# Seven block products for eight in the feed-forward stage of a two-layer decoder trunk

## The chip, the cores and the metric

The kernel runs as one program on one core of one Trainium2 chip. The metric is device time in microseconds (us) of one execution: the median of the runs shown.

## The reference

Two layers over 256 tokens of width 2048, all in float32. A layer has a mixer (one input projection, a causal convolution branch, an attention branch, gates, an output projection), then a SwiGLU feed-forward part of hidden width 5632, then a gated embedding. The change lies in the feed-forward part and in how weights are loaded:

```python
hf = rmsnorm(x, norm_ffn_g[i])
gate, up = jnp.split(hf @ w_gate_up[i], 2, axis=-1)
x = x + (jax.nn.silu(gate) * up) @ w_down[i]
```

## The kernel before, in words

**Tiling.** The 256 tokens are two blocks of 128 (`b` in 0, 1); the contraction is cut into tiles of 128 (`k`), and the output columns into chunks of 512. One weight chunk `w[g]` holds four k-tiles of 512 columns, 128 x 2048 numbers, and comes by one DMA.

**Precision.** Every float32 operand is split into a high part `h` (rounded to float32r by ACT) and a low part `l` (the rest, by DVE), and a product is three matmuls: high x high, high x low, low x high (lines 168 to 170). For activations, which stand transposed as the stationary operand, `halves` (line 183) does the split; for weights, which stream, `load` (line 131) does it: L147 on ACT writes `wh`, L148 on DVE writes `wl`, each 128 x 1024, two of each for a DMA. Both kinds have 4 buffers, the raw weights 3 (of 128 x 2048).

**A chunk.** `chunk` (line 154) loads one weight group after another and issues, for each k-tile and token block, three matmuls into two PSUM banks: 12 matmuls for each half group ("block" below), 24 for a group of four k-tiles. Between groups `run()` (line 81) issues what has been queued meanwhile, for instance the transposes of a finished hidden tile.

**Feed-forward.** The loop at line 676 goes over three parts of 3, 4 and 4 column chunks of the hidden width. In a part, each chunk `c` takes one gate and one up projection over 16 k-tiles (96 matmuls each), the gate's activation (L682, L683) and product (L686), and queues `operand` (line 202), which turns the hidden chunk by eight transposes (L199) and splits it (L186, L187) into four k-tiles. After a part's chunks, the down projection runs for each of four column chunks over 4 x nch k-tiles and is added to the residual stream `xt` (L666). Ahead of the stage, while the output projection runs (line 668 on), `advance` queues `Norm.turn` (line 226), which turns a finished column block of `xt` and splits it with the norm's gains (L189 on ACT, L190 on DVE).

**Order.** The program is written in one sequence; the tile framework's scheduler decides the order on each engine at build time, and each engine works strictly in that order. SP issues all weight DMAs in order, each as soon as a raw buffer is free.

Of the kernel before, what the change touches and what calls it, by code (L numbers as in the profile page):

```python
# [10 lines left out]
F32 = mybir.dt.float32  # L11
# [5 lines left out]
P = 128  # L17
# [17 lines left out]
PAIRS = 23  # L35
CONV = 7
# [7 lines left out]
def trunk(ctx, tc, xT, xR, pT, wI, wF, wC, wA, wOut, wGU, wD, wPG, wPP, vec, bF, gF, out):  # L44
# [4 lines left out]
    raws = pool("raws", 3)  # L49
    whs = pool("whs", 4)  # L50
    wls = pool("wls", 4)
    tmps = pool("tmps", 8)
# [78 lines left out]
    def load(src, n=2048, hook=None):  # L131
        raw = raws.tile([P, 2048], F32, tag="raw", name=f"raw{next(uid)}")
        if hook is None:
            nc.sync.dma_start(raw[:, :n], src)
        else:
            nc.sync.dma_start(raw[:, :512], src[:, :512])
            nc.sync.dma_start(raw[:, 512:1024], src[:, 512:1024])
            hook()
            nc.sync.dma_start(raw[:, 1024:], src[:, 1024:])
        parts = []  # L140
        step = 1024 if hook is None else 512
        for lo in range(0, n, 1024):
            h = whs.tile([P, 1024], F32R, tag="wh", name=f"wh{next(uid)}")
            l = wls.tile([P, 1024], F32R, tag="wl", name=f"wl{next(uid)}")
            for o in range(0, 1024, step):
                e = o + step
                act.activation(h[:, o:e], raw[:, lo + o : lo + e], AF.Copy)  # L147
                dve.tensor_tensor(l[:, o:e], raw[:, lo + o : lo + e], h[:, o:e].bitcast(F32), op=ALU.subtract)  # L148
            parts.append((h, l))
        return parts  # L150
# [3 lines left out]
    def chunk(groups, xs, acc, hook=None):  # L154
        n = sum(len(ks) for _, ks in groups)
        done = 0
        for src, ks in groups:
            parts = load(src, 512 * len(ks), hook)
            hook = None
            while not all(k in xs for k in ks):  # L160
                assert turns or tasks
                run()
            for j, k in enumerate(ks):
                h, l = parts[j // 2]
                cs = slice((j % 2) * 512, (j % 2 + 1) * 512)
                for b in range(2):
                    xh, xl = xs[k][:, b * P : (b + 1) * P], xs[k][:, S + b * P : S + (b + 1) * P]
                    pe.matmul(acc[b], lhsT=xh, rhs=h[:, cs], start=(done == 0), stop=False)  # L168
                    pe.matmul(acc[b], lhsT=xh, rhs=l[:, cs], start=False, stop=False)  # L169
                    pe.matmul(acc[b], lhsT=xl, rhs=h[:, cs], start=False, stop=(done == n - 1))  # L170
                done += 1
# [30 lines left out]
    def operand(xs, k0, src):  # L202
        for half, pt in turned(src):
            o = pair(F32R)
            halves(o, pt)
            for kk in range(2):
                xs[k0 + 2 * half + kk] = o[:, kk, :]

    class Norm:


        def __init__(self, gcol):
            self.gcol, self.xs = gcol, {}
            self.ss = small(8)
# [11 lines left out]
        def turn(self, n):  # L226
            for half, pt in turned(lambda b: xt[:, b, n * 512 : (n + 1) * 512]):
                o = pair(F32R)
                for kk in range(2):
                    k = 4 * n + 2 * half + kk  # L230
                    halves(o[:, kk, :], pt[:, kk, :], self.gain(k))
                    self.xs[k] = o[:, kk, :]
# [47 lines left out]
    def take(q, lo=0, hi=4):  # L280
        for k in range(lo, hi):
            if k % 2 == 0:
                o = pair(F32R)
                norm.xs[4 * q + k], norm.xs[4 * q + k + 1] = o[:, 0, :], o[:, 1, :]
            halves(
                norm.xs[4 * q + k], xin[q].rearrange("p a b -> p (a b)")[:, k * S : (k + 1) * S],
                norm.gain(4 * q + k),
            )
# [23 lines left out]
    for i in range(L):  # L312
# [7 lines left out]
        def project(c, hook=None):  # L320
            return chunk(by_four(wI[i, c]), norm.xs, banks(), hook)
# [164 lines left out]
        def scores(hd):  # L486
# [39 lines left out]
            def pv():  # L526
# [8 lines left out]
                o_att[hd] = o_pairs[hd // 2][:, hd % 2, :]  # L535
                halves(o_att[hd], po[:, :S])
# [20 lines left out]
        def conv_norm():  # L557
# [30 lines left out]
            def finish(c):  # L588
# [8 lines left out]
                o_conv[c] = r["o"][:, c % 2, :]  # L597
                halves(o_conv[c], t)
# [31 lines left out]
        def attended(n):  # L630
            return chunk(by_four(wA[i, n], 2), o_att, banks())
# [24 lines left out]
        for n in range(N4):  # L656
            t = gate_a[n]
            gated_by(t, chunk(by_four(wC[i, n], 2), o_conv, banks()))
# [9 lines left out]
        norm = Norm(g_ffn)  # L668
        for n in range(N4):
            residual(n, chunk(by_four(wOut[i, n]), merged, banks()))  # L670
            advance(norm, n)
# [4 lines left out]
        for part, nch in enumerate(FFN_PARTS):  # L676
            hid = {}
            for c in range(c0, c0 + nch):
                pg = chunk(by_four(wGU[i, 2 * c]), norm.xs, banks())
                t = [tmp() for _ in range(2)]  # L680
                for b in range(2):
                    act.activation(t[b], pg[b], AF.Sigmoid, scale=norm.r(b))  # L682
                    dve.scalar_tensor_tensor(t[b], pg[b], norm.r(b), t[b], op0=ALU.mult, op1=ALU.mult)  # L683
                pu = chunk(by_four(wGU[i, 2 * c + 1]), norm.xs, banks())
                for b in range(2):
                    dve.scalar_tensor_tensor(t[b], pu[b], norm.r(b), t[b], op0=ALU.mult, op1=ALU.mult)  # L686
                turns.append(lambda c=c, t=t, hid=hid: operand(hid, 4 * c, lambda b: t[b]))
            for n in range(N4):
                groups = [(wD[i, n, c], range(4 * c, 4 * c + 4)) for c in range(c0, c0 + nch)]
                residual(n, chunk(groups, hid, banks()))  # L690
                if part == len(FFN_PARTS) - 1:
                    advance(after, n)
            c0 += nch
            if part == len(FFN_PARTS) - 2:
# [4 lines left out]
                ps = {k: po[:, k, :] for k in range(2)}  # L699
# [5 lines left out]
        def embed(n):  # L705
            return chunk([(wPP[i, n], range(2))], ps, [bank_ms() for _ in range(2)])
# [6 lines left out]
        for n in range(N4):  # L713
            e = embed(n)
            acc = chunk(by_four(wPG[i, n]), norm.xs, banks())
# [84 lines left out]
```

## Time and profile before

| | |
|---|---|
| median of 3 runs | 2903.79 us (2902.66 to 2904.2) |
| the profiled execution's own time | 2902.9 us |
| its span, first to last instruction | 2900.8 us |
| mean granted TensorE clock | 0.998 |
| busy: TensorE (PE), DVE, ACT | 99%, 60%, 47% of the span |
| DMA, mean over the span | 187 GB/s |

Spans of the profile are read against 2900.8 us; the 2.1 us around the span belong to every execution. A matmul's listed duration (0.39 us) is longer than the distance to the next one, since matmuls are pipelined; what one costs is the distance between starts.

### The profile page before, as it was taken

The numbers are of one execution on the slowest core, as the hardware profiler recorded it, in microseconds if no ns is written. First come the engines' busy times: TensorE is split into PE (matmuls) and PEld (weight loads), VectorE is DVE, ScalarE is ACT, GpSimd is POOL, SyncE is SP. The second block draws the span as 40 slices with busy tenths as digits, with TensorE's granted clock in tenths as the row PEclk, the third lists the DMA queues.
The fourth block names the chain that finished last, engine by engine and source line by source line (L and its number), as shares of the span: only waits on it lengthen the run. The fifth ranks groups of instructions, "written<-read, shape, count | busy, mean of one in ns | idle before, by whom it ended". The sixth has DMA issues, their size and how long they took to land.

```text
span 2900.8 us, 32675 instructions
## 1 busy us (share of the span) xinstructions
PE 2876.6 (99%) x13004; PEld 2381.2 (82%) x13004; DVE 1751.8 (60%) x2264; ACT 1356.2 (47%) x1642; POOL 9.5 (0%) x40
## 2 busy tenths in 40 slices
PE   8999999999999999999999999999999999999998
PEld 6888888888888888888888888888888888888886
DVE  5997745555555555555569966465555555455554
ACT  5445744444444434445554456444443444344444
POOL 0000000000000000000000000000000000000000
PEclk9999999999999999999999999999999999999999
DMA  7554455555555555555555544555555555555553
GB/s 271 174 186 163 170 193 189 189 185 188 193 188 189 192 193 193 189 188 183 186 181 181 183 166 174 190 188 189 188 189 188 190 191 189 198 190 188 189 195 139
DMA packets 77048, 543.11 MB, mean 187 GB/s; under 512 B 8800, under 2 KB 9056, under 8 KB 12256
## 3 DMA queue, kind: packets, MB, share of 16 engines
q1 hardware_dynamic: 76896, 541.04, 53.2%
q8 instruction: 101, 1.65, 0.2%
q14 instruction: 51, 0.42, 0.0%
HBM read 538.91 MB, written 2.10 MB: 187 GB/s over the span
## 4 chain that ended last, share of the span: by engine, by line
PE 94%; DVE 4%; DMA 1%; ACT 0%; issue 0%; SPq 0%; POOL 0%; ACTq 0%; POOLq 0%; DVEq 0%
PE mm L170 30%; PE mm L168 30%; PE mm L169 30%; PE ms L199 2%; DVE pair L336 2%; DVE wl L148 2%; DMA xt<-in_xR_dram 1%; PE ms L495 0%; PE ms L170 0%; PE ms L169 0%; PE ms L168 0%; PE ms L531 0%; DMA pair<-in_xT_dram 0%; ACT tmp L221 0%; PE ms L497 0%
## 5 line engine op out<-in xcount | busy, mean ns | idle before, releaser
L148 DVE TENSOR_TENSOR wl<-raw,wh 128x1024 fp32r<-128x1024 f32 (+1 forms) x1018 | 1242.0, 1222 | 1073.9 <-ACT wh L147 1072.7
L147 ACT ACTIVATE wh<-raw 128x1024 fp32r<-128x1024 f32 (+1 forms) x1018 | 1076.6, 1058 | 1414.9 <-PE mm L170 1356.7
L168 PE MATMUL mm<-wh,pair 128*128 128x512 f32 x4032 | 1579.6, 392 | 9.3 <-ACT wh L147 9.3
L170 PE MATMUL mm<-wh,pair 128*128 128x512 f32 x4032 | 1571.8, 390 | 0.0
L169 PE MATMUL mm<-wl,pair 128*128 128x512 f32 x4032 | 1571.1, 390 | 0.5 <-DVE wl L148 0.5
L168 PEld LDWEIGHTS mm<-wh,pair 128*128 128x128 f32 x4032 | 758.0, 188 | 164.4 <-ACT wh L147 10.5
L170 PEld LDWEIGHTS mm<-wh,pair 128*128 128x128 f32 x4032 | 757.7, 188 | 158.5
L169 PEld LDWEIGHTS mm<-wl,pair 128*128 128x128 f32 x4032 | 758.1, 188 | 156.7 <-DVE wl L148 1.8
L336 DVE SCALAR_TENSOR_TENSOR pair<-pair,vecs,pair 128x256 f32<-128x256 f32 x480 | 201.1, 474 | 0.0
L187 DVE TENSOR_TENSOR pair<-ms,pair 128x512 fp32r<-128x512 f32 (+1 forms) x76 | 45.1, 626 | 1.4 <-ACT pair L186 1.3
L189 ACT ACTIVATE pair<-ms,vecs 128x256 fp32r<-128x256 f32 x80 | 33.9, 466 | 16.4 <-DVE pair L190 16.4
L666 DVE TENSOR_TENSOR xt<-xt,mm 128x512 f32<-128x512 f32 x64 | 40.9, 680 | 0.0
L682 ACT ACTIVATE tmp<-mm,rt 128x512 f32<-128x512 f32 x44 | 30.0, 690 | 21.7 <-PE mm L170 21.7
L186 ACT ACTIVATE pair<-ms 128x512 fp32r<-128x512 f32 (+1 forms) x76 | 37.9, 540 | 0.6 <-PE ms L532 0.6
L683 DVE SCALAR_TENSOR_TENSOR tmp<-mm,rt,tmp 128x512 f32<-128x512 f32 x44 | 31.4, 751 | 9.9 <-ACT tmp L682 9.9
L221 ACT ACTIVATE tmp<-xt 128x512 f32<-128x512 f32 x56 | 34.6, 618 | 5.0 <-DVE xt L721 4.2
L190 DVE SCALAR_TENSOR_TENSOR pair<-ms,vecs,pair 128x256 fp32r<-128x256 f32 x80 | 35.2, 479 | 2.6 <-ACT pair L189 1.4
L199 PEld LDWEIGHTS ms<-ident,tmp 128*128 128x128 f32 x272 | 31.7, 141 | 4.5
L199 PE MATMUL ms<-ident,tmp 128*128 128x128 f32 x272 | 35.2, 272 | 0.0
L686 DVE SCALAR_TENSOR_TENSOR tmp<-mm,rt,tmp 128x512 f32<-128x512 f32 x44 | 30.9, 743 | 0.0
L510 ACT ACTIVATE tmp<-tmp,small 128x128 f32<-128x128 f32 (+1 forms) x32 | 14.5, 454 | 19.5 <-DVE small L509 19.3
L622 ACT ACTIVATE pair<-mm,rt 128x512 f32<-128x512 f32 x28 | 18.5, 684 | 5.9 <-PE mm L170 5.9
(146 smaller groups left out, 571.0 us busy)
## 6 DMA issues: line engine op xcount, KB each, us to landing
raw<-in_wGU_dram SPq DMA_DIRECT2D x176, 1024.0 KB, 4.7
raw<-in_wI_dram SPq DMA_DIRECT2D x143, 1024.0 KB, 4.7
raw<-in_wD_dram SPq DMA_DIRECT2D x88, 1024.0 KB, 4.7
raw<-in_wOut_dram SPq DMA_DIRECT2D x32, 1024.0 KB, 4.7
raw<-in_wPG_dram SPq DMA_DIRECT2D x32, 1024.0 KB, 4.7
raw<-in_wA_dram SPq DMA_DIRECT2D x16, 1024.0 KB, 4.7
raw<-in_wC_dram SPq DMA_DIRECT2D x16, 1024.0 KB, 4.7
raw<-in_wPP_dram SPq DMA_DIRECT2D x8, 512.0 KB, 3.2
```

The costliest lines, as they stand in the source:

```text
L147: act.activation(h[:, o:e], raw[:, lo + o : lo + e], AF.Copy)
L148: dve.tensor_tensor(l[:, o:e], raw[:, lo + o : lo + e], h[:, o:e].bitcast(F32), op=ALU.subtract)
L168: pe.matmul(acc[b], lhsT=xh, rhs=h[:, cs], start=(done == 0), stop=False)
L169: pe.matmul(acc[b], lhsT=xh, rhs=l[:, cs], start=False, stop=False)
L170: pe.matmul(acc[b], lhsT=xl, rhs=h[:, cs], start=False, stop=(done == n - 1))
L186: act.activation(hi, src, AF.Copy)
L187: dve.tensor_tensor(lo, src, hi.bitcast(F32), op=ALU.subtract)
L190: dve.scalar_tensor_tensor(lo, src, scale, hi.bitcast(F32), op0=ALU.mult, op1=ALU.subtract)
L199: pe.transpose(pt[:, kk * S + b * P : kk * S + (b + 1) * P], src(b)[:, c : c + P], ident)
L221: act.activation(tmp(), xt[:, b, n * 512 : (n + 1) * 512], AF.Square, accum_out=self.ss[:, b * 4 + n : b * 4 + n + 1],)
L336: dve.scalar_tensor_tensor(cv[c], u[c][:, j : j + S], w, cv[c], op0=ALU.mult, op1=ALU.add,)
L666: dve.tensor_tensor(xc, xc, acc[b], op=ALU.add)
```

## The change

In the first group of each product, four k-tiles and two column chunks are taken together as a 2 x 2 block matrix product: token blocks x halves of two k-tiles, halves of two k-tiles x column chunks. It is computed with seven block products in place of eight (the Strassen scheme in Winograd's form). That takes sums of weight blocks, of operand blocks and of results.

- `fast_chunks` (new, line 211) does two column chunks at once. Four half groups of weights (`a11`, `a21`, `a22`, `a12`) are held as raw tiles; three more weight operands are made from them by four 128 x 1024 additions on DVE, partly in place. Each of the seven operands is split like a weight tile and multiplied by 6 matmuls (2 k-tiles x 3) with one of the operand combinations `B11` to `N4X`. The other groups run as before, two k-tiles at a time, by `go()`. Four products (`p1`, `q5`, `q6`, `q7`) go to the small PSUM pool, are combined in SBUF (L254 to L258), and are added to the four long sums at the end (L268 to L272).
- `Fast` (new, line 304) holds the operand side: `take` copies the two turned halves out of PSUM, `make` forms four combinations on DVE (L323) and splits all eight 128 x 256 blocks at once (two of L332 on ACT, two of L333 on DVE). The tiles that `take` and `make` fill first come from the raw pool.
- `fast_chunks` is called for gate and up of every hidden chunk but the first of a layer (10 calls in a layer), and for two pairs of down chunks in each part (6 calls in a layer).
- All weights now come in half groups of 128 x 1024 with a DMA of their own; 7 raw buffers of that size in place of 3 of double size; 9 `tmp` buffers for 8.

```diff
-    raws = pool("raws", 3)
+    raws = pool("raws", RAWS)
-    tmps = pool("tmps", 8)
+    tmps = pool("tmps", 9)
...
+    def fast_chunks(fast, w1, w2, xs, ks):
+        nk = 4 * len(ks)
+        p1, q5, q6, q7 = (Sum(2, bank_ms) for _ in range(4))
+        c11, c12, c21 = (Sum(2 + nk, bank_mm) for _ in range(3))
+        c22 = Sum(nk, bank_mm)
...
+        def product(to, which, raw):
+            h, l = split(raw)
+            xh, xl = fast(which)
+            for kk in range(2):
+                to.add(xh(kk), xl(kk), h[:, kk, :], l[:, kk, :])
...
+        a11, a21 = fetch(w1[0][:, :1024]), fetch(w2[0][:, :1024])
+        a22, a12 = fetch(w2[0][:, 1024:]), fetch(w1[0][:, 1024:])
+        s3 = raws.tile([P, 2, 512], F32, tag="raw", name=f"sum{next(uid)}")
+        product(p1, B11, a11)
+        add(s3, a11, a21)
+        add(a21, a21, a22)
+        product(q5, M1, a21)
+        go()
+        product(q7, T3, s3)
+        add(a11, a11, a21)
+        product(q6, T2, a11)
+        u1, u3, u4, u5 = (tmp() for _ in range(4))
+        act.activation(u1, p1.t, AF.Copy)
+        dve.tensor_tensor(u4, u1, q6.t, op=ALU.subtract)
+        dve.tensor_tensor(u3, u4, q7.t, op=ALU.add)
+        add(u4, u4, q5.t)
+        add(u5, u3, q5.t)
+        go()
+        product(c21, N4X, a22)
+        go()
+        product(c11, B21, a12)
+        go()
+        add(a12, a12, a11)
+        product(c12, B22, a12)
+        while len(left) > 2 * len(ks):
+            go()
+        add(u1, u1, c11.t)
+        add(u4, u4, c12.t)
+        go(2 * len(ks))
+        dve.tensor_tensor(u3, c21.t, u3, op=ALU.subtract)
+        dve.tensor_tensor(u5, c22.t, u5, op=ALU.subtract)
+        return (u1, u4), (u3, u5)
...
+        def make(self):
...
+            sub(M1, B11, B12, ALU.subtract)
+            sub(T2, M1, B22, ALU.add)
+            sub(T3, B22, B12, ALU.subtract)
+            sub(N4X, B21, T2, ALU.subtract)
...
+            for t in self.f:
...
+                act.activation(h, t, AF.Copy)
+                dve.tensor_tensor(l, t, h.bitcast(F32), op=ALU.subtract)
...
-        norm = Norm(g_ffn)
+        norm = Norm(g_ffn, fast=True)
...
-                pg = chunk(by_four(wGU[i, 2 * c]), norm.xs, banks())
...
+                    g, t = fast_chunks(norm.fast, w1, w2, norm.xs, (4, 8, 12))
...
-                residual(n, chunk(groups, hid, banks()))
...
+                y = fast_chunks(
+                    fast_hid, wD[i, n][c0 : c0 + nch], wD[i, n + 1][c0 : c0 + nch], hid,
+                    range(4 * c0 + 4, 4 * c0 + 4 * nch, 4),
+                )
```

**The order at three places.** Names carry their number, so that one tile can be followed.

First, TensorE in the gate and up call of a part's second hidden chunk (here the first part of the first layer): the end of a block of the long sums, the eight transposes of the part's first hidden chunk, a product for `c21`, and the next block.

```order
L177 MATMUL mm1000_5426<-wh1012_5470,pair867_4762 128x512
L295 MATMUL ms1014_5486<-ident_86,tmp981_5373 128x128
...
L295 MATMUL ms1015_5492<-ident_86,tmp982_5374 128x128
L175 MATMUL mm1022_5514<-wh1020_5510,pair834_4591 128x512
...
L177 MATMUL mm1022_5514<-wh1020_5510,pair835_4592 128x512
L175 MATMUL mm999_5422<-wh1024_5523,pair897_4924 128x512
L175 MATMUL mm1000_5426<-wh1024_5523,pair897_4924 128x512
L176 MATMUL mm999_5422<-wl1025_5524,pair897_4924 128x512
```

Between the transposes and the next block, which needs `wh1024` and `wl1025`, stand the 6 matmuls of `c21`. On ACT, at the same place:

```order
L140 ACTIVATE wh1012_5470<-raw1011_5468 128x1024
L140 ACTIVATE wh1020_5510<-raw987_5387 128x1024
L314 ACTIVATE fast923_5059<-ms1014_5486 128x512
L314 ACTIVATE fast923_5059<-ms1015_5492 128x512
L332 ACTIVATE pair1016_5502<-fast923_5059 128x1024
L332 ACTIVATE pair1018_5506<-fast924_5060 128x1024
L140 ACTIVATE wh1024_5523<-raw1023_5521 128x1024
L140 ACTIVATE wh1026_5539<-raw988_5389 128x1024
```

The two copies and the two splits of `Fast` stand ahead of `wh1024`; on DVE the four combinations and two splits stand ahead of `wl1025` likewise. Before, two L186 stood at such a place.

Second, ACT at the norm ahead of the stage, where the first column block of `xt` is turned. Before:

```order
L147 ACTIVATE wh740_4404<-raw739_4402 128x1024
L147 ACTIVATE wh742_4408<-raw739_4402 128x1024
L221 ACTIVATE tmp726_4342,small699_4185<-xt_82 128x512
L221 ACTIVATE tmp727_4344,small699_4185<-xt_82 128x512
L147 ACTIVATE wh745_4438<-raw744_4436 128x1024
L147 ACTIVATE wh747_4442<-raw744_4436 128x1024
L189 ACTIVATE pair736_4387<-ms735_4382,vecs_83 128x256
```

and now (on TensorE the eight transposes into `ms830` and `ms831` are followed at once by the matmuls of `wh837`):

```order
L140 ACTIVATE wh826_4539<-raw825_4537 128x1024
L376 ACTIVATE tmp820_4527,small789_4362<-xt_82 128x512
L376 ACTIVATE tmp821_4529,small789_4362<-xt_82 128x512
L317 ACTIVATE fast787_4360<-ms830_4569,vecs_83 128x2x128 x2
L317 ACTIVATE fast787_4360<-ms831_4576,vecs_83 128x2x128 x2
L332 ACTIVATE pair832_4587<-fast787_4360 128x1024
L332 ACTIVATE pair834_4591<-fast788_4361 128x1024
L140 ACTIVATE wh837_4597<-raw836_4595 128x1024
```

Before, four weight blocks (`wh740` to `wh747`) that the matmuls behind the transposes read were ahead of the turn; now none is.

Third, DVE in a later gate and up call, from the first result of `q6` (`ms1081`) to the split of the weight block `wl1103`, which TensorE reads 36 matmuls and eight transposes after `q6`:

```order
L255 TENSOR_TENSOR tmp1084_5813<-tmp1082_5811,ms1081_5804 128x512
L141 TENSOR_TENSOR wl1100_5884<-raw1063_5741,wh1099_5883 128x1024
L256 TENSOR_TENSOR tmp1083_5812<-tmp1084_5813,ms1078_5792 128x512
L241 TENSOR_TENSOR raw1063_5741<-raw1063_5741,raw1060_5735 128x1024
L241 TENSOR_TENSOR tmp1084_5813<-tmp1084_5813,ms1070_5761 128x512
L241 TENSOR_TENSOR tmp1085_5814<-tmp1083_5812,ms1070_5761 128x512
L283 TENSOR_TENSOR pair1090_5843<-ms1089_5838,pair1090_5843 128x2x256
L283 TENSOR_TENSOR pair1092_5851<-ms1091_5846,pair1092_5851 128x2x256
L141 TENSOR_TENSOR wl1103_5896<-raw1101_5893,wh1102_5895 128x1024
```

Before, only weight splits and the gate's two products stood there.

## Rows read from the trace of the kernel before

**Rows 1.** The page's part 1: busy time of each engine, its share of the span, and its instructions.

```profile
PE 2876.6 (99%) x13004; PEld 2381.2 (82%) x13004; DVE 1751.8 (60%) x2264; ACT 1356.2 (47%) x1642; POOL 9.5 (0%) x40
```

**Rows 2.** Totals over the whole span, by engine and line it waited for: us in total, times, longest. All engines but the DMA queue.

```profile
ACT wh L147 <- PE mm L170: 1356.7, 844, 2.4
DVE wl L148 <- ACT wh L147: 1072.7, 841, 2.1
...
PE mm L168 <- ACT wh L147: 9.3, 3, 7.4
```

**Rows 3.** Busy time by stretch, here the feed-forward stage of the first layer: start and end of the stretch, its length, then busy us (and instructions) of PE, PEld, DVE, ACT and POOL, the granted TensorE clock, the DMA share and GB/s.

```profile
580.00:1180.00 600.00, 600.00 (x2692) 497.60 (x2692) 319.35 (x306) 256.89 (x274) 0.69 (x1) 1.00 0.55 190
```

**Rows 4.** Instructions in order of time in that stage, one block of twelve matmuls with the work beside it: start, us, engine, line, operation, tiles, idle time before it and what ended that.

```profile
899.95 0.39 PE L168 MATMUL mm<-wh,pair 128*128 128x512 f32 x1
...
900.83 1.06 ACT L147 ACTIVATE wh<-raw 128x1024 fp32r<-128x1024 f32 x1 [1.66 <-PE mm L170]
...
901.92 1.23 DVE L148 TENSOR_TENSOR wl<-raw,wh 128x1024 fp32r<-128x1024 f32 x1 [1.49 <-ACT wh L147]
...
902.67 0.39 PE L168 MATMUL mm<-wh,pair 128*128 128x512 f32 x1
```

**Rows 5.** Groups of instructions by line and shape: out<-in, shapes, count | busy us in total, mean ns of one | idle before them. (L148 is the low part of a weight tile, L147 the high part, L336 a step of the depthwise convolution, L660 and L562 plain adds of two tiles in SBUF, L187 and L186 the low and high part of a turned operand, L686 the product of gate and up.)

```profile
L148 DVE TENSOR_TENSOR wl<-raw,wh 128x1024 fp32r<-128x1024 f32 x1014 | 1239.3, 1224 | 1073.8 <-ACT wh L147 1072.7
L147 ACT ACTIVATE wh<-raw 128x1024 fp32r<-128x1024 f32 x1014 | 1074.3, 1060 | 1414.9 <-PE mm L170 1356.7 <-issue 26.6 <-DVE pair L336 14.4
...
L187 DVE TENSOR_TENSOR pair<-ms,pair 128x512 fp32r<-128x512 f32 x60 | 38.4, 682 | 0.0
...
L189 ACT ACTIVATE pair<-ms,vecs 128x256 fp32r<-128x256 f32 x80 | 33.9, 466 | 16.4 <-DVE pair L190 16.4
...
L186 ACT ACTIVATE pair<-ms 128x512 fp32r<-128x512 f32 x60 | 32.0, 585 | 0.0
...
L686 DVE SCALAR_TENSOR_TENSOR tmp<-mm,rt,tmp 128x512 f32<-128x512 f32 x44 | 30.9, 743 | 0.0
...
L660 DVE TENSOR_TENSOR pair<-pair,pair 128x512 f32<-128x512 f32 x16 | 10.3, 684 | 0.0
...
L562 DVE TENSOR_TENSOR tmp<-tmp,pair 128x256 f32<-128x256 f32 x12 | 5.1, 423 | 0.3
```

**Rows 6.** The chain of waits in order of time, in the convolution stretch of the first layer, where DVE works back to back: start, us, what, count.

```profile
89.98 2.27 DVE wl L148 x2
92.25 2.05 DVE pair L336 x6
```

**Rows 7.** TensorE in order of time around the eight transposes (L199) that turn the first hidden tile of the feed-forward stage.

```profile
668.45 1.04 PE L199 MATMUL ms<-ident,tmp 128*128 128x128 f32 x8
669.24 0.47 PE L168 MATMUL mm<-wh,pair 128*128 128x512 f32 x1
```

**Rows 8.** ACT in order of time at the same place.

```profile
668.65 1.06 ACT L147 ACTIVATE wh<-raw 128x1024 fp32r<-128x1024 f32 x1 [1.67 <-PE mm L170]
669.62 1.06 ACT L186 ACTIVATE pair<-ms 128x512 fp32r<-128x512 f32 x2
```

**Rows 9.** ACT in order of time where the norm ahead of the feed-forward stage turns its first column block (L189, four halves).

```profile
556.33 1.06 ACT L147 ACTIVATE wh<-raw 128x1024 fp32r<-128x1024 f32 x1 [1.67 <-PE mm L170]
557.30 0.82 ACT L189 ACTIVATE pair<-ms,vecs 128x256 fp32r<-128x256 f32 x2
559.08 0.87 ACT L189 ACTIVATE pair<-ms,vecs 128x256 fp32r<-128x256 f32 x2 [0.96 <-DVE pair L190]
559.93 1.06 ACT L147 ACTIVATE wh<-raw 128x1024 fp32r<-128x1024 f32 x1
```

**Rows 10.** TensorE in order of time at the start of the program.

```profile
7.35 0.80 PE L168 MATMUL mm<-wh,pair 128*128 128x512 f32 x1 [7.35 <-ACT wh L147]
...
12.38 0.63 PE L170 MATMUL mm<-wh,pair 128*128 128x512 f32 x1
...
16.22 0.53 PE L170 MATMUL mm<-wh,pair 128*128 128x512 f32 x1
16.58 0.40 PE L168 MATMUL mm<-wh,pair 128*128 128x512 f32 x1
16.82 0.39 PE L169 MATMUL mm<-wl,pair 128*128 128x512 f32 x1
```

**Rows 11.** TensorE in order of time at the only later place where it waits.

```profile
30.52 0.73 PE L168 MATMUL mm<-wh,pair 128*128 128x512 f32 x2 [1.52 <-ACT wh L147]
31.78 0.50 PE L169 MATMUL mm<-wl,pair 128*128 128x512 f32 x1 [0.53 <-DVE wl L148]
...
34.90 0.39 PE L168 MATMUL mm<-wh,pair 128*128 128x512 f32 x1
...
35.58 0.39 PE L168 MATMUL mm<-wh,pair 128*128 128x512 f32 x1
```

**Rows 12.** The page's part 6, DMA issues: tiles, queue, count, KB each, median us from issue to landing.

```profile
raw<-in_wGU_dram SPq DMA_DIRECT2D x176, 1024.0 KB, 4.7
...
raw<-in_wPP_dram SPq DMA_DIRECT2D x8, 512.0 KB, 3.2
```

**Rows 13.** What the DMA queue (SP) waited for over the whole span: us in total, times, longest.

```profile
SPq L134 <- DVE wl L148: 2404.9, 468, 12.1
```

More of the change, by code (lines that the diff above doesn't have):

```diff
@@ L35 @@
 PAIRS = 23
+RAWS = 7
 CONV = 7
@@ L128, in trunk, with fetch @@
     nc.gpsimd.memset(lf, 0.0)
[L131 to L139, printed above, removed]
-        parts = []
[L141 to L148, printed above, removed]
+    def fetch(src):
+        raw = raws.tile([P, 2, 512], F32, tag="raw", name=f"raw{next(uid)}")
+        nc.sync.dma_start(raw.rearrange("p k n -> p (k n)"), src)
+        return raw
@@ new lines, in split, with fetch_first @@
+    def split(raw):
+        h = whs.tile([P, 2, 512], F32R, tag="wh", name=f"wh{next(uid)}")
+        l = wls.tile([P, 2, 512], F32R, tag="wl", name=f"wl{next(uid)}")
+        act.activation(h, raw, AF.Copy)
+        dve.tensor_tensor(l, raw, h.bitcast(F32), op=ALU.subtract)
+        return h, l
+    def fetch_first(src, hook):
+        parts = []
+        for half in range(2):
+            raw = raws.tile([P, 2, 512], F32, tag="raw", name=f"raw{next(uid)}")
+            h = whs.tile([P, 2, 512], F32R, tag="wh", name=f"wh{next(uid)}")
+            l = wls.tile([P, 2, 512], F32R, tag="wl", name=f"wl{next(uid)}")
+            c = half * 1024
+            if half == 0:
+                for k in range(2):
+                    nc.sync.dma_start(raw[:, k, :], src[:, k * 512 : (k + 1) * 512])
+                hook()
+            else:
+                nc.sync.dma_start(raw.rearrange("p k n -> p (k n)"), src[:, c : c + 1024])
+            for k in range(2):
+                act.activation(h[:, k, :], raw[:, k, :], AF.Copy)
+                dve.tensor_tensor(l[:, k, :], raw[:, k, :], h[:, k, :].bitcast(F32), op=ALU.subtract)
@@ L155, in chunk, with plain, await_x @@
+    def plain(sums, xs, k0, parts, n=2):
+        h, l = parts
+        for kk in range(n):
+            for b in range(2):
+                xh, xl = xs[k0 + kk]
+                sums[b].add(xh(b), xl(b), h[:, kk, :], l[:, kk, :])
+    def await_x(xs, ks):
+        while not all(k in xs for k in ks):
+            assert turns or tasks
+            run()
+    def chunk(groups, xs, bank, hook=None):
         n = sum(len(ks) for _, ks in groups)
-        done = 0
+        sums = [Sum(n, bank) for _ in range(2)]
@@ L157, in chunk @@
         for src, ks in groups:
[L158 to L171, printed above, removed]
+            if hook is not None:
+                parts = fetch_first(src, hook)
+                hook = None
+            else:
+                parts = [split(fetch(src[:, o * 512 : (o + 2) * 512])) for o in range(0, len(ks), 2)]
@@ L203, in operand @@
+    def operand(xs, k0, src, fast=None):
         for half, pt in turned(src):
+            if fast is not None:
+                fast.take(half, pt)
+                continue
             o = pair(F32R)
@@ L206, in operand, with __init__ @@
             for kk in range(2):
-                xs[k0 + 2 * half + kk] = o[:, kk, :]
+                xs[k0 + 2 * half + kk] = by_blocks(o[:, kk, :])
+        if fast is not None:
+            xs.update(zip(range(k0, k0 + 4), fast.column_tiles()))
     class Norm:
-        def __init__(self, gcol):
-            self.gcol, self.xs = gcol, {}
+        def __init__(self, gcol, fast=False):
+            self.gcol, self.xs, self.tiles = gcol, {}, {}
+            self.fast = Fast() if fast else None
             self.ss = small(8)
@@ L227, in turn @@
             for half, pt in turned(lambda b: xt[:, b, n * 512 : (n + 1) * 512]):
+                if n == 0 and self.fast:
+                    self.fast.take(half, pt, [self.gain(2 * half + kk) for kk in range(2)])
+                    if half == 1:
+                        self.xs.update(enumerate(self.fast.column_tiles()))
+                    continue
                 o = pair(F32R)
@@ L698, in trunk @@
                 halves(po, pin)
-                ps = {k: po[:, k, :] for k in range(2)}
+                ps = {k: by_blocks(po[:, k, :]) for k in range(2)}
         norm = after
@@ L705, in embed @@
         def embed(n):
-            return chunk([(wPP[i, n], range(2))], ps, [bank_ms() for _ in range(2)])
+            return chunk([(wPP[i, n], range(2))], ps, bank_ms)
         if last:
@@ L714, in trunk @@
             e = embed(n)
-            acc = chunk(by_four(wPG[i, n]), norm.xs, banks())
+            acc = chunk(by_four(wPG[i, n]), norm.xs, bank_mm)
             for b in range(2):
```

130 lines of the change are left out of this document (102 added, 28 removed).

## The prediction

> **What bounds the kernel now.** Read the engines' totals first: TensorE is busy 99% of the span, DVE 60%, ACT 47% [rows 1]. Then who waited for whom: ACT's weight splits wait 1356.7 us for TensorE to give a buffer back, DVE's wait 1072.7 us for ACT, and TensorE waits 9.3 us in all, 7.4 of them at the start [rows 2]. So the helpers run ahead until TensorE lets them go on, and time is what the matmuls take. In the feed-forward stage of the first layer TensorE is busy 600.00 of 600 us and DVE 319.35 [rows 3]. One block of twelve matmuls goes from 899.95 to 902.67, which is 0.2267 us a matmul; beside it stand one ACT split, 1.06 us after 1.66 us of waiting, and one DVE split, 1.23 us after 1.49 us [rows 4]. DVE starts 0.03 us after ACT ends: a handover costs about that, and I count 0.04.
>
> **Matmuls removed.** A call does its first group with 7 x 6 = 42 matmuls in place of 48. There are 10 calls for gate and up and 6 for down in a layer, 32 in all, so 192 matmuls go: 192 x 0.2267 = **43.5 us**. This is the whole gain, and it counts only where TensorE stays fed.
>
> **DVE and ACT on average.** A call adds three splits (1.224 us), four sums of the same size and eight additions of 128x512 (0.684, or 0.682 out of PSUM): 3.7 + 4.9 + 5.5 = 14 us on DVE, 450 us over 32 calls [rows 5]. No row shows a 128x1024 sum in float32; the split, which reads two such tiles and writes one, is the nearest. With some 20 us for the operand combinations, DVE comes to 1752 + 470 = 2220 us, under 80%. ACT gains three splits and a copy, 3.8 us a call, and stays near 52%. Both are covered on average. Call by call DVE has, for gate and up, 19 splits, 4 sums, 8 additions, 4 products and 2 turned halves: 23.2 + 4.9 + 5.5 + 3.0 + 1.4 = 38 us, against 186 x 0.2267 = 42.2 for TensorE, plus transposes. For a down call of four chunks it is 36.4 against 42.2. For one of three chunks it is 31.5 against 138 x 0.2267 = 31.3: no slack, in four calls of the program. But 1.224 is the price of a lone split; back to back two take 2.27 [rows 6], 1.135 each, which makes 29.8 there. I take 0.5 us lost in each of the four, 2 in all; the ends are 0 and 6.
>
> Within a call the hardest place is behind `q6`, whose result DVE must wait for (the third piece of order). From there to the end of the split `wl1103` stand 0.68 + 1.22 + 0.68 + 1.22 + 0.68 + 0.68 + 2 x 0.68 + 1.22 = 7.7 us of DVE; TensorE has 36 matmuls, 8.2 us, and eight transposes before it needs that. It holds by about a microsecond, so I charge nothing; were it short, each call would pay the difference.
>
> **The operand combinations, six parts.** Here the cover is gone. A part's first hidden chunk is turned inside the call for the second, and ACT's and DVE's work on all eight blocks stands in one lump ahead of the next weight block (the first piece). Count from the first transpose. Eight transposes take 0.79 us, the last ends at 1.04 [rows 7]; `c21` gives 6 x 0.2267 = 1.36, so TensorE runs dry at 2.15. ACT: the two copies, 0.585 each, 1.06 for two [rows 5, 8], run from 0.66 to 1.77. DVE: three of the four combinations need the second copy; at 0.42 (the 128x256 sum, [rows 5]) they end at 3.07. ACT splits the first tile by 2.87, the second, which needs the last combination, from 3.11 to 4.17, and only then makes `wh1024`, by 5.23. TensorE restarts at 5.25: **3.1 us** idle. It does two matmuls (to 5.7) and wants `wl1025`; DVE has done the two operand splits by 4.25 and 5.4 and that one by 6.55: **0.9 us** more. Together 4.0 us a part, 24 us in six. If every operation overlaps with the next as in rows 6, it is 3.4; with 0.1 us a handover, 4.6.
>
> **The same at the norm, twice.** Before, four weight blocks stood ready when the block was turned, ACT splitting weights until just before it [rows 9]; now none does (the second piece). TensorE runs dry at 0.79. The four copies, 0.82 for two [rows 9], end at 2.30, the combinations at 3.60, ACT's splits at 3.40 and 4.70, `wh837` at 5.74: **5.0 us** idle, then two matmuls and 0.9 more for `wl838`. 5.9 us a norm, 11.8 in two (10.4 to 12.8).
>
> **The clock.** TensorE starts after 7.35 us without work and its first 18 matmuls, to 16.58, stand 0.427 us apart (12.38 to 16.22 are nine steps), which is the lower of its two levels; then 0.23 [rows 10]. Later it waits once, 1.52 and 0.53 us close together, and matmuls behind that are 0.227 apart (34.90 to 35.58): no fall [rows 11]. The new gaps of 3.1 and 5.0 us lie between these rows. The sum takes no fall; a full one costs 18 x 0.2 = 3.6 us. The Trainium skill ("TensorE: Matmul & The Clock Gate", Why this matters for your kernels) speaks against such a change: it asks that TensorE have no long idle gaps between bursts, since it then goes back to half clock. By that, the sum below rises by 7.2 us if the norm's gaps count and by 29 if all eight do; rows 11 are too short a gap to show it.
>
> **Loads.** Weights come by 512 KB in place of 1024; the one row of that size lands in 3.2 us, a large one in 4.7 [rows 12]. TensorE uses 512 KB in 2.72 us, so two in flight suffice. A call holds up to five of seven raw tiles, which leaves two. SP has time for twice the issues, waiting 2404.9 us for raw buffers now [rows 13]. I charge nothing; the bound is one landing, 3.2 us, in each of the six parts' first turns, 19 us, where all seven are held, and most of that would lie inside the gap counted already.
>
> **The sum.** -43.5 + 24 + 11.8 + 2 = -5.7 us on the profiled execution's 2902.9, that is 2897.2. Its own time lies 0.9 us below the median shown, so the median would be 2898.1; the overlaps of rows 6 should shave a little from the gaps, and I say **2897**. The case's own range is 2889 to 2905: the gaps at their low and high prices (-5, +5), the tight calls (-2, +4). What can be told from no change is 0.2%, 5.8 us: below 2898.0 is faster, above 2909.6 slower. The forecast stands at that edge.
>
> **Rivals.**
> - *All is covered* and the full 43.5 us are kept: 2860. The order speaks against it: each engine works in its written order, and nothing else is ahead of TensorE there. 7%.
> - *The clock falls at the norm's two gaps*: 2897 + 7 = 2904, no change that can be told. For it, the gap of 5.0 us follows only transposes; against it, the fall is known only from a start that was 7.35 us. 17%.
> - *The clock falls at all eight gaps*, the case that comes out slower: 2897 + 29 = 2926. It decides from the fourth gap on (4 x 3.6 = 14.4 against the 12.6 us to 2909.6). Against it stands the gap of 1.5 us that left the clock alone [rows 11], and that the parts' gaps are 3.1 us. 11%.
> - *DVE is late in every call*: the place behind `q6` has a microsecond of slack, and sums in place may cost more than splits. With 0.5 us lost in each of the 28 other calls, 2911. For it, DVE at 85 to 100% of a call; against it, the back-to-back price. 13%.
> - That the change does not do what it says can be left out: TensorE's order holds 192 matmuls fewer.
>
> **How the numbers follow.** The forecast has 52%, split by the edge into 32 faster and 20 same. Faster: 32 + 7 + a few = 42%. Same: 20 + 17 and a third of the late DVE = 40%. Slower: 11 and the rest of the late DVE = 18%. The range leaves out full cover below and the fall at all gaps above and takes in the others: 2886 to 2915.
>
> **What would show it.** In the profile after, TensorE waits about 29 us for ACT's weight split in eight places, about 3 us in six and 5 in two, and some 7 us for DVE's split right behind them; it waited 0 for them in the same stage before. DVE is busy near 2200 us, matmuls of 512 columns number 192 fewer, and 0.227 apart on both sides of a gap. Wrong it would be by waits in most of the 32 calls (DVE late), matmuls 0.427 apart after a gap (clock), waits for a raw tile's DMA, or no waits at all.

## The result: slower by 0.3%

| | before | after |
|---|---|---|
| median, same chip | 2903.85 us (2901.83 to 2904.45, 8 runs) | 2912.14 us (2910.46 to 2913.43, 8 runs) |
| ratio after / before, 95% interval | | 1.003 (1.0019 to 1.004) |
| the profiled execution's own time | 2902.9 us | 2912.83 us |
| its span | 2900.8 us | 2911.1 us |
| mean granted TensorE clock | 0.998 | 0.990 |

The forecast was 2897. The time lies inside the range (2886 to 2915) and on the other side of no change.

### The profile page after: what moved, and what is told of

It is laid out like the page before. It is cut to its first block, busy times and chain, and to the rows that moved or that the text cites. A ratio compares the mean times of both kernels' runs of the same rounds, so it can differ in the third digit from the quotient of the medians.

```text
span 2911.1 us, 34422 instructions
## 1 busy us (share of the span) xinstructions
PE 2856.5 (98%) x12812; PEld 2355.9 (81%) x12812; DVE 2164.5 (74%) x2772; ACT 1484.5 (51%) x1786; POOL 9.5 (0%) x40
## 4 chain that ended last, share of the span: by engine, by line
PE 94%; DVE 4%; ACT 1%; DMA 1%; issue 1%; SPq 0%; POOL 0%; ACTq 0%; POOLq 0%; DVEq 0%
PE mm L176 28%; PE mm L177 28%; PE mm L175 28%; PE ms L177 2%; PE ms L175 2%; PE ms L176 2%; PE ms L295 2%; DVE wl L141 1%; DVE pair L498 1%; DMA xt<-in_xR_dram 0%; DVE fast L323 0%; PE ms L657 0%; DVE pair L333 0%; DMA raw<-in_wI_dram 0%; PE ms L693 0%
## 5 line engine op out<-in xcount | busy, mean ns | idle before, releaser
L141 DVE TENSOR_TENSOR wl<-raw,wh 128x1024 fp32r<-128x1024 f32 x1078 | 1307.2, 1222 | 651.6 <-ACT wh L140 641.8
L140 ACT ACTIVATE wh<-raw 128x1024 fp32r<-128x1024 f32 x1078 | 1139.8, 1060 | 1220.2 <-PE mm L177 1045.5
L175 PE MATMUL mm<-wh,pair 128*128 128x512 f32 x3712 | 1461.9, 394 | 35.3 <-ACT wh L140 27.8
L176 PE MATMUL mm<-wl,pair 128*128 128x512 f32 x3712 | 1455.8, 392 | 3.5 <-DVE wl L141 3.5
L177 PE MATMUL mm<-wh,pair 128*128 128x512 f32 x3712 | 1454.5, 392 | 0.8 <-DVE pair L283 0.8
L175 PEld LDWEIGHTS mm<-wh,pair 128*128 128x128 f32 x3712 | 701.0, 189 | 181.2 <-ACT wh L140 31.3
L176 PEld LDWEIGHTS mm<-wl,pair 128*128 128x128 f32 x3712 | 702.5, 189 | 154.4 <-DVE wl L141 10.2
L177 PEld LDWEIGHTS mm<-wh,pair 128*128 128x128 f32 x3712 | 701.9, 189 | 148.3 <-DVE pair L283 1.7
L241 DVE TENSOR_TENSOR raw<-raw,raw 128x1024 f32<-128x1024 f32 x96 | 117.1, 1220 | 1.2
L177 PE MATMUL ms<-wh,pair 128*128 128x512 f32 x288 | 112.1, 389 | 0.0
L175 PE MATMUL ms<-wh,pair 128*128 128x512 f32 x288 | 112.1, 389 | 0.0
L176 PE MATMUL ms<-wl,pair 128*128 128x512 f32 x288 | 112.1, 389 | 0.0
L177 PEld LDWEIGHTS ms<-wh,pair 128*128 128x128 f32 x288 | 54.1, 188 | 11.2
L175 PEld LDWEIGHTS ms<-wh,pair 128*128 128x128 f32 x288 | 54.1, 188 | 11.2
L140 ACT ACTIVATE wh<-sum 128x1024 fp32r<-128x1024 f32 x32 | 34.0, 1062 | 50.7 <-PE mm L177 50.7
L376 ACT ACTIVATE tmp<-xt 128x512 f32<-128x512 f32 x56 | 34.8, 622 | 17.2 <-DVE xt L830 11.1
L141 DVE TENSOR_TENSOR wl<-sum,wh 128x1024 fp32r<-128x1024 f32 x32 | 38.9, 1217 | 0.0
```

Of the source, the lines that this page charges most:

```text
L140: act.activation(h, raw, AF.Copy)
L141: dve.tensor_tensor(l, raw, h.bitcast(F32), op=ALU.subtract)
L175: pe.matmul(self.t, lhsT=xh, rhs=wh, start=start, stop=False)
L176: pe.matmul(self.t, lhsT=xh, rhs=wl, start=False, stop=False)
L177: pe.matmul(self.t, lhsT=xl, rhs=wh, start=False, stop=self.left == 0)
L241: add = lambda o, a, b: dve.tensor_tensor(o, a, b, op=ALU.add)
```

## The profile after

The page's part 1, which answers to [rows 1] (PEld is TensorE's loading of the stationary operand, which overlaps PE):

```profile
PE 2856.5 (98%) x12812; PEld 2355.9 (81%) x12812; DVE 2164.5 (74%) x2772; ACT 1484.5 (51%) x1786; POOL 9.5 (0%) x40
```

TensorE has 192 instructions fewer, as it should. But 192 matmuls at 0.2267 us are 43.5 us, and its busy time fell by only 20.1. So the remaining matmuls were listed 23.4 us longer in all; that is the first trace of the clock. (The end of a listed duration reaches some 0.17 us into each wait, which makes a small part of it.) In the changed kernel L175 to L177 are the three matmuls, L140 and L141 the high and low part of a weight block, L159 the first such split of the program, L283 the low part of a turned operand and L295 the transposes. What TensorE waited for over the whole span (engine and line <- what it waited for: us in total, times, longest), against [rows 2]:

```profile
PE mm L175 <- ACT wh L140: 27.8, 9, 4.4
PE mm L175 <- ACT wh L159: 7.4, 1, 7.4
PE mm L176 <- DVE wl L141: 3.5, 9, 0.7
PE mm L177 <- DVE pair L283: 0.8, 2, 0.4
```

Line 2 is the start of the program. Of line 1, one wait of 3.71 stands at 29.88, where [rows 11] had 1.52; the other eight, 24.1 us, are the eight places that the prediction named. Here is TensorE in order of time at the first norm (start, us, instruction, and in brackets the idle time before it), where it had no wait before:

```profile
557.49 1.04 PE L295 MATMUL ms<-ident,xt 128*128 128x128 f32 x8
562.91 1.22 PE L175 MATMUL mm<-wh,pair 128*128 128x512 f32 x2 [4.39 <-ACT wh L140]
564.37 0.79 PE L176 MATMUL mm<-wl,pair 128*128 128x512 f32 x1 [0.23 <-DVE wl L141]
564.96 0.63 PE L177 MATMUL mm<-wh,pair 128*128 128x512 f32 x1
...
567.52 0.61 PE L175 MATMUL mm<-wh,pair 128*128 128x512 f32 x1
567.95 0.42 PE L176 MATMUL mm<-wl,pair 128*128 128x512 f32 x1
568.21 0.39 PE L177 MATMUL mm<-wh,pair 128*128 128x512 f32 x1
```

Read the starts, not the durations. From the first transpose at 557.49 to the matmul at 568.21 pass 10.72 us. The transposes (0.79) and 11 matmuls at 0.2267 each make 3.28 of that: 7.4 us are lost. The brackets show 4.62 of them. The rest is in the steps: from 564.96 to 567.52 matmuls start 0.427 apart, as at the program's start [rows 10], so on the lower of the two clock levels (1.2 GHz), and from 568.21 on 0.23 apart, the higher one (2.4 GHz). A part, in the same view (there TensorE waits behind the six matmuls of `c21`):

```profile
684.71 0.40 PE L177 MATMUL mm<-wh,pair 128*128 128x512 f32 x1
687.67 1.22 PE L175 MATMUL mm<-wh,pair 128*128 128x512 f32 x2 [2.56 <-ACT wh L140]
689.11 0.79 PE L176 MATMUL mm<-wl,pair 128*128 128x512 f32 x1 [0.23 <-DVE wl L141]
...
693.97 0.53 PE L176 MATMUL mm<-wl,pair 128*128 128x512 f32 x1
694.34 0.40 PE L177 MATMUL mm<-wh,pair 128*128 128x512 f32 x1
```

Fifteen matmuls, 3.4 us, take 9.63: 6.2 lost, of which the brackets show 2.79. Not every part is alike. In the second one the clock falls later:

```profile
886.41 0.73 PE L175 MATMUL mm<-wh,pair 128*128 128x512 f32 x2 [2.56 <-ACT wh L140]
887.86 0.50 PE L176 MATMUL mm<-wl,pair 128*128 128x512 f32 x1 [0.72 <-DVE wl L141]
...
888.97 0.63 PE L175 MATMUL mm<-wh,pair 128*128 128x512 f32 x1
...
891.95 0.53 PE L176 MATMUL mm<-wl,pair 128*128 128x512 f32 x1
892.32 0.39 PE L177 MATMUL mm<-wh,pair 128*128 128x512 f32 x1
```

The first two matmuls behind this gap take 0.73 us together against 1.22 above: still the high level. At 888.97 it is the low one. Because TensorE uses the first block faster, it catches up with DVE's split and waits 0.72 for it where it had waited 0.23.

Stretches around the norm and the first four parts (start and end, length, busy us and count of PE, PEld, DVE, ACT, POOL, then the granted clock, DMA share, GB/s); the long one answers to [rows 3]:

```profile
580.00:1180.00 600.00, 590.76 (x2610) 486.75 (x2610) 474.97 (x496) 305.22 (x330) 0.69 (x1) 0.99 0.55 188
555.00:570.00 15.00, 10.38 (x39) 7.81 (x38) 8.69 (x11) 8.53 (x11) 0.00 (x0) 0.77 0.40 125
684.00:696.00 12.00, 9.21 (x27) 6.54 (x26) 10.66 (x12) 7.69 (x9) 0.00 (x0) 0.72 0.63 200
883.00:895.00 12.00, 8.73 (x30) 6.40 (x29) 10.71 (x13) 8.18 (x9) 0.00 (x0) 0.86 0.63 210
1145.00:1157.00 12.00, 9.21 (x27) 6.56 (x26) 10.66 (x12) 7.99 (x9) 0.00 (x0) 0.72 0.65 211
2128.00:2140.00 12.00, 9.06 (x33) 6.57 (x32) 10.81 (x12) 7.77 (x8) 0.00 (x0) 0.86 0.67 225
```

The granted clock lies between 0.72 and 0.86 in each; in the stretches of the other norm and parts it was 0.74, 0.74 and 0.86. It fell at all eight places. The Trainium skill ("TensorE: Matmul & The Clock Gate", Why this matters for your kernels) warns that idle gaps between bursts put TensorE back to half clock; these rows agree, and at gaps of 2.56 us.

What TensorE waits for at the norm, on ACT (two lines of its lump and the weight splits behind them, the first of which TensorE needs) and on DVE, against [rows 9]:

```profile
558.13 1.57 ACT L317 ACTIVATE fast<-ms,vecs 128x256 f32<-128x256 f32 x4 [4.44 <-PE ms L295]
559.73 2.19 ACT L332 ACTIVATE pair<-fast 128x1024 fp32r<-128x1024 f32 x2
561.82 3.88 ACT L140 ACTIVATE wh<-raw 128x1024 fp32r<-128x1024 f32 x4
```

```profile
560.82 2.36 DVE L333 TENSOR_TENSOR pair<-fast,pair 128x1024 fp32r<-128x1024 f32 x2
```

ACT had stood idle for 4.44 us until the transposes came, with the weights of the next blocks in SBUF (the last of their loads was issued at 549.15, and no load there took over 6.2 us): in its order the four copies and two splits come first. It then takes 3.7 us for them and 1.06 for the block that TensorE wants. Nothing here is slow; it is in the wrong place.

**Where the 10.3 us of span came from.** Take at each place the time between two starts less 0.2267 us a matmul. The norms lose 7.4 and 7.8, the parts 6.2, 5.5, 6.2, 4.9, 6.7 and 4.9, the start 1.4 more than before; all excess in the program rose by 53.6. Less the 43.5 us of matmuls that gives +10.1.

## Experiments

All of them compute the whole result. Theory A: the eight gaps cost what they idle, and the clock falls at each on top. Against it: that the loads cost, that DVE is late throughout the calls (D), that the gaps cost their idle time alone (G), and others named where they are tested. Every ratio is to the kernel before on the same chip, 2903.26 to 2903.84 us.

**The new loading alone.** `fast_chunks` and `Fast` are not used; weights come by 512 KB.

```diff
-        norm = Norm(g_ffn, fast=True)
+        norm = Norm(g_ffn)
...
-                    g, t = fast_chunks(norm.fast, w1, w2, norm.xs, (4, 8, 12))
...
+                g = chunk(by_four(w1), norm.xs, bank_mm)
...
-                y = fast_chunks(
+                residual(n, chunk(groups, hid, bank_mm))
```

> The new loading alone (512 KB a DMA, seven raw tiles, nine tmp tiles), all products with eight block products as before; the result is the reference's. Theory A (the loss lies in eight gaps of TensorE, each lengthened by a fall of the clock behind it): only the start costs more, some 1.5 us by the first 40 us of the two traces, so 2905 (2903 to 2907). Rival L (smaller loads land later, 4.2 us for 3.2, and cost a little everywhere): a good part of the 8 us shows here, 2908 or more.

Measured: 2904.12 us, ratio 1.0001 (0.9992 to 1.0009). The loads cost nothing that can be told. Yet in the changed kernel they landed little sooner than large ones (tiles, queue, count, KB, median us to landing; [rows 12] had 4.7 for the double size and 3.2 for the few small ones):

```profile
raw<-in_wGU_dram SPq DMA_DIRECT2D x352, 512.0 KB, 4.2
raw<-in_wI_dram SPq DMA_DIRECT2D x287, 512.0 KB, 3.9
raw<-in_wD_dram SPq DMA_DIRECT2D x176, 512.0 KB, 4.3
```

**Each half of the change alone.** In the first kernel only gate and up take seven products, in the second only the down projection; the other half is written as in the experiment above.

> Seven products for eight in the 20 gate and up calls alone; the down projections as before. 120 matmuls go, 27.2 us. Theory A: two gaps at the norms remain, 7.4 us each with their slow matmuls, the six of the parts are gone: 2903.9 - 27.2 + 14.8 + 1.5 = 2893 (2890 to 2896). Rival D (every call loses a little because DVE is late, 51.8 us over 32 calls = 1.6 us a call): 2903.9 - 27.2 + 32 = 2909.

> Seven products for eight in the 12 down calls alone; gate and up as before. 72 matmuls go, 16.3 us. Theory A: the six gaps of the parts remain and are longer, since no product stands between the transposes and the next weight block any more (1.36 us more each: some 4 us and 0.7 behind it) and the clock falls at each (about 2.5 us): 2903.9 - 16.3 + 6 x 7.2 + 1.5 = 2932 (2926 to 2938), slower than before by 1%. Rival D: 2903.9 - 16.3 + 12 x 1.6 = 2907.

Measured: gate and up alone 2890.86 us, ratio 0.9957 (0.9943 to 0.997), faster; down alone 2933.35, ratio 1.0102 (1.0086 to 1.0117), slower by more than the whole change. TensorE's largest new wait in the two, the first with 20 calls and two gaps, the second with 12 calls and six (one more of each count is the start):

```profile
PE mm L175 <- ACT wh L140: 12.2, 3, 4.4
```

```profile
PE mm L175 <- ACT wh L140: 26.6, 7, 3.9
```

The time goes with the gaps and not with the calls. D, which charged the calls and so wanted 2909 and 2907, falls. In the second kernel a part's gap is 3.9 us and not 2.56, since without `c21`'s six matmuls (1.36 us) TensorE runs dry sooner: the two halves are not additive.

**The operands made, all products with eight.** `Fast` is taken and made as in the change. The plain matmuls read its four turned blocks as their operand; nothing reads the four combinations. TensorE keeps its 13004 instructions.

```diff
-                    g, t = fast_chunks(norm.fast, w1, w2, norm.xs, (4, 8, 12))
...
+                g = chunk(by_four(w1), norm.xs, bank_mm)
...
-                y = fast_chunks(
+                residual(n, chunk(groups, hid, bank_mm))
```

> The lump alone: the first operand group of each norm and part is still taken, combined and split eight blocks at once, but every product is done with eight block products; the result is the reference's. Theory A (gap plus fall of the clock, wherever the lump stands): 2904.1 of the loads alone + 2 x 7.4 + 6 x 7.6 (what the down calls alone showed a part) = 2964 (2956 to 2970). Rival H (the gaps come from the calls' raw tiles being held, so that weights land late): no such tiles are held here, near 2906.

Measured: 2962.57 us, ratio 1.0204 (1.0189 to 1.0219). The eight lumps by themselves cost 59.2 us (2962.57 - 2903.42), with TensorE's matmuls as before and the weights loaded as in the first experiment. H, which wanted 2906, falls. It is more than the changed kernel's 53.6 for the reason just given: a part's gap is 3.9 us here too.

**The gaps filled.** In each lump TensorE gets matmuls on constants behind the eight transposes, into a bank that nobody reads. ACT and DVE work as in the change, and the wait for the weight block is the same; only TensorE is not idle.

```diff
             if half == 1:
+                idle = bank_ms()
+                for _ in range(10 if gains is None else 19):
+                    pe.matmul(idle, lhsT=nsel[:, 4, :], rhs=nsel[:, :4, :]..., start=True, stop=True)
                 self.make()
```

> The changed kernel with 10 idle matmuls (19 at the norm) of constants into an unread PSUM bank right behind the eight transposes of each gap: TensorE works through the gap and nothing else moves. Theory A: the gaps keep their length but the clock no longer falls at the eight places; about 2 us each come back: 2896 (2892 to 2900), granted clock about 0.997. Rival G (the gaps alone cost it and the clock's fall is hidden behind the next wait): 2912 (2910 to 2914).

Measured: 2897.62 us, ratio 0.9979 (0.997 to 0.9988). TensorE at the norm (L321 are the 19 idle matmuls), and the stretches of the norm and the first part:

```profile
557.62 1.04 PE L295 MATMUL ms<-ident,xt 128*128 128x128 f32 x8
558.41 4.57 PE L321 MATMUL ms<-nsel 128*128 128x512 f32 x19
563.05 0.73 PE L175 MATMUL mm<-wh,pair 128*128 128x512 f32 x2
564.50 0.51 PE L176 MATMUL mm<-wl,pair 128*128 128x512 f32 x1 [0.72 <-DVE wl L141]
564.85 0.40 PE L177 MATMUL mm<-wh,pair 128*128 128x512 f32 x1
```

```profile
555.00:570.00 15.00, 14.21 (x66) 11.19 (x65) 9.65 (x11) 8.68 (x12) 0.00 (x0) 1.00 0.44 130
684.00:696.00 12.00, 11.00 (x48) 8.46 (x47) 10.81 (x11) 8.29 (x9) 0.00 (x0) 1.00 0.72 235
```

The weight block's first matmul starts 5.43 us behind the first transpose in either kernel (563.05 - 557.62; 562.91 - 557.49), so the lump is as late as ever. But the clock stays at 1.00, and 14.5 us come back (2912.14 - 2897.62), 1.8 for each of the eight gaps. G, which wanted 2912 here, falls.

**Half as many idle matmuls**, 5 and 10 in place of 10 and 19.

> As the filled gaps, with half the idle matmuls: 5 behind the parts' transposes, 10 behind the norms'. Idle left: 2.56 - 5 x 0.227 = 1.4 us in the parts, 4.39 - 2.27 = 2.1 in the norms. If a gap of 1.4 to 2.1 us leaves the clock alone, as the 1.52 us at the start of the kernel before did: 2898, as filled. If the norms' two gaps still bring it down: 2902. If all eight do: 2912, as unfilled.

Measured: 2906.12 us, ratio 1.0008 (0.9999 to 1.0017), between what was expected with falls nowhere or at the norms and with falls everywhere. Gaps of 1.41 us and 0.72 close behind remain in the parts, of 2.11 and 0.73 at the norms. Five of the stretches, the last a norm:

```profile
683.00:693.00 10.00, 7.87 (x34) 5.87 (x33) 8.81 (x10) 6.84 (x8) 0.00 (x0) 1.00 0.67 204
880.00:890.00 10.00, 7.87 (x28) 5.75 (x27) 8.81 (x8) 6.86 (x7) 0.00 (x0) 0.83 0.71 236
1142.00:1152.00 10.00, 7.87 (x27) 5.68 (x26) 8.81 (x8) 6.79 (x7) 0.00 (x0) 0.83 0.70 236
2123.00:2133.00 10.00, 7.87 (x34) 5.90 (x33) 8.81 (x9) 6.84 (x8) 0.00 (x0) 1.00 0.70 229
559.00:569.00 10.00, 7.21 (x24) 5.52 (x25) 8.10 (x7) 5.91 (x6) 0.00 (x0) 0.83 0.75 219
```

The clock fell at three of six like gaps (0.83) and not at the other three (1.00), and at both norms. That is the one execution profiled, which took 2904.0 us, the shortest of ten, at a mean granted clock of 0.996. The other nine show 0.994 or 0.995, so the falls need not be tied to these places. I found no row that tells a gap with a fall from one without.

**The lump behind three weight blocks.** The copies, sums and splits are put, on ACT's and DVE's queues, behind the splits of the next three weight blocks; the transposes stay ahead of those blocks' matmuls. No work is removed.

```diff
+    def behind(blocks, lump):
+        parts = [split(fetch(src)) for src in blocks]
+        a, d = (getattr(i, "ins", i) for i in newest)
+        with tc.issue_after(a), tc.issue_after(d):
+            lump()
+        return parts
...
+        if late is not None:
+            go(1)
+            three = [left.popleft() for _ in range(3)]
+            for parts, (_, sums, k0) in zip(behind([src for src, _, _ in three], late), three):
+                plain(sums, xs, k0, parts)
...
-            residual(n, chunk(by_four(wOut[i, n]), merged, bank_mm))
+            lump = turns.pop() if n == 1 else None
+            residual(n, chunk(by_four(wOut[i, n]), merged, bank_mm, lump=lump))
```

> The changed kernel with each lump queued on ACT and DVE behind the splits of the next three weight blocks (18 of 24 matmuls would do), and a part's first turn moved to the end of the second hidden chunk's call; nothing is left out. Theory A: no gap, no fall, the 43.5 us come through but for about 1 us in the tight down calls: 2903.9 - 43.5 + 1 = 2861 (2859 to 2865). Rival D (DVE at 85 to 100% of a call takes its own toll): 2870 or more.

Measured: 2862.65 us, ratio 0.986 (0.9845 to 0.9875), faster than both kernels. TensorE's waits, apart from a first one of 7.5 at the start, and the long stretch of [rows 3]:

```profile
PE mm L186 <- ACT wh L141: 2.2, 1, 2.2
PE mm L187 <- DVE wl L142: 0.9, 1, 0.9
PE mm L188 <- DVE pair L314: 0.8, 2, 0.4
```

```profile
580.00:1180.00 600.00, 599.61 (x2689) 496.64 (x2688) 491.74 (x515) 315.47 (x339) 0.69 (x1) 1.00 0.58 195
```

In this kernel L186 to L188 are the matmuls, L141 and L142 the splits of a weight block, L314 the low part of a turned operand, L326 the transposes, L348 and L363 the copies and splits of `Fast`. The first two lines of the waits are one place near the start, the third is two down calls of three chunks. TensorE is full again with DVE at 82%. At the norm, ACT now has the lump between weight splits, and TensorE goes on from the last transpose to the next matmul (start, us, engine, instruction):

```profile
559.32 1.06 ACT L141 ACTIVATE wh<-raw 128x1024 fp32r<-128x1024 f32 x1 [1.66 <-PE mm L188]
562.43 1.57 ACT L348 ACTIVATE fast<-ms,vecs 128x256 f32<-128x256 f32 x4 [2.05 <-PE ms L326]
564.03 2.19 ACT L363 ACTIVATE pair<-fast 128x1024 fp32r<-128x1024 f32 x2
```

```profile
561.80 1.04 PE L326 MATMUL ms<-ident,xt 128*128 128x128 f32 x8
562.59 0.48 PE L186 MATMUL mm<-wh,pair 128*128 128x512 f32 x1
```

**The same for the parts alone**; the norm's piece of that diff is left away.

> The same for the six parts only; the norms' two lumps stay as in the changed kernel. Theory A: 2861 + 2 x 7.4 = 2876 (2873 to 2879). Rival N (the norm's gaps cost nothing beyond their idle time): 2861 + 2 x 5 = 2871.

Measured: 2877.36 us, ratio 0.991 (0.9893 to 0.9926). Against the kernel above, the two norms cost 14.7 us, 7.35 each, where the starts in the changed kernel gave 7.4 and 7.8. N, which wanted 2871, falls. The six parts then cost 2912.14 - 2877.36 = 34.8, or 5.8 each.

**The lump behind one block** in place of three.

```diff
-            three = [left.popleft() for _ in range(3)]
+            three = [left.popleft()]
```

> Each lump queued behind one weight block in place of three: 12 matmuls, 2.72 us, of cover. In the parts some 4.0 us are then to be covered (no product stands there at the call's end), so 1.3 idle and 0.9 behind it; at the norms 1.7 and 0.9: 2862.7 + 6 x 2.2 + 2 x 2.6 = 2881 with no fall of the clock; 2897 with a fall of 2 us at all eight.

Measured: 2895.04 us, ratio 0.997 (0.9959 to 0.9982). It is near the number expected with falls everywhere, and for another reason: the clock fell at three of the eight places only. Each part lost 3.5 us even without a fall, more than expected, 2.5 at the gap (1.2 idle, then 0.72) and 1.0 in small waits some 15 us later. One block is not enough cover, and I had sized what it leaves wrongly. Two of the parts, without a fall and with one:

```profile
699.00:709.00 10.00, 8.10 (x34) 6.04 (x34) 9.62 (x9) 5.91 (x6) 0.00 (x0) 1.00 0.70 232
895.00:905.00 10.00, 8.10 (x28) 5.92 (x27) 8.38 (x9) 5.91 (x6) 0.00 (x0) 0.83 0.70 229
```

## Why the prediction was wrong

By its own steps:

- *What bounds the kernel*: right. TensorE does, and what feeds it has room everywhere but at the lumps.
- *Matmuls removed*, 43.5 us: right. With the lumps covered, the kernel is 40.8 us faster (2903.42 - 2862.65). Of the 2.7 us that are missing, the waits in two tight down calls are 1.1 by the starts; the rest lies in many small steps.
- *DVE and ACT on average*: right. DVE is busy 2164.5 us (forecast 2220), ACT 51%. A sum in place takes 1220 ns, the price of a split that was taken for it [rows 5]. The place behind `q6` shows no wait. The four tight down calls show two waits of 0.4 us: 0.8 (1.1 by the starts) for the 2 charged, each in a layer's first down call.
- *The gaps*: right in place and kind, and nearly in size. The brackets count idle time from the end of the last listed duration: 2.56 us in a part, 4.39 at a norm, and 0.23 to 0.72 for DVE's split. By the starts, as the forecast counted, TensorE ran dry for 2.7 us in a part (forecast 3.1) and 4.6 at a norm (5.0), as four copies of ACT took 1.57 us and two splits 2.19; DVE's split cost 1.0 more where the clock was still up (886.41 to 887.86 less two matmuls; forecast 0.9). All eight without their clock cost 2912.14 - 2862.65 - 14.5 = 35.0 us, by three runs. The prediction charged 24 + 11.8 = 35.8.
- *Loads*: nothing, right, though the landing time taken for the bound, 3.2 us, was 3.9 to 4.3.
- *The clock*: here it failed. The step was "The sum takes no fall", a term put at nothing, chosen between a gap of 1.52 us that left the clock alone and a start of 7.35 us that did not [rows 10, 11]. It fell at all eight gaps. With the clock held up by idle matmuls, the kernel measures 2897.62, which is the predicted 2897; with the falls, 2912.14. These 14.5 us are nearly the whole miss of 15.1.

So the third rival came true, the fall at all eight gaps, which had 11%. Its price was twice too high: 1.8 us a gap and not 3.6, which had been read off the 18 matmuls after the program's start. In the changed kernel the low level holds for fewer matmuls, 7 to 13 in the places shown, and where it begins at once TensorE waits less for DVE's split (0.23 for 0.72). With 8 x 1.8 in place of 8 x 3.6 that rival would have said 2911, but 1.8 is read from these same runs.

The chance was also chosen badly. The parts' gap of 3.1 us lay nearer to the 1.52 that left the clock alone, and I let nearness decide; but [rows 11] were one place, where TensorE had hardly begun to run. The Trainium skill ("TensorE: Matmul & The Clock Gate", Why this matters for your kernels) spoke for the fall and was weighed against that one place.

The second rival, a fall at the norms alone, is out by the windows at the parts; "DVE is late in every call" by the two halves; full cover came to 2862.65 where the order was changed, against the 2860 given for it.

## What to carry to other kernels

An idle gap of TensorE costs its length and, in these runs at every gap of 2.56 us or more, a stretch at half clock behind it, so price both, and read a gap's loss from the starts of the matmuls around it rather than from the wait. When a change adds work to the engines that feed TensorE, their average load says little: look in each engine's order for places where the new work stands in one lump ahead of the next block, and queue it behind as many ready blocks as it lasts (here three blocks, 8.2 us of matmuls, hid a lump of 3.7 us on ACT; one block, 2.7 us, did not; two were not tried). The same arithmetic was 0.3% slower or 1.4% faster by that alone.

## What the runs showed of the hardware

- In the one profiled execution of each kernel, the clock fell at six of six gaps of 2.56 us and at both of 4.39; with 1.41 + 0.72 us of idle it fell at three of six, and with 1.2 + 0.72 at two of six; at the norms it fell at both gaps of 2.11 + 0.73 and at one of two of 1.65 + 0.72. In the kernel with the new loads alone, 2.2 us and 0.8 near the start were followed by a granted clock of 0.66 from 30 to 40 us. What decides in the short gaps stays open: the same gap in the same run did both.
- The fall does not always stand right behind the gap: at 886.41 two matmuls and more ran at the high level first, and the low one began 2.5 us later.
- Idle matmuls that nobody reads kept the granted clock at 1.00 and were worth 14.5 us.
- DMAs of half the size, 149492 packets in place of 77048, left the time unchanged (1.0001) with seven half buffers for three whole ones.
